# Restaging the output projection of a two-layer hybrid decoder: other buffers, an earlier fetch, a later transpose

## The chip, the cores and the metric

The kernel runs on one core of one Trainium2 chip. The core has five engines, each with an instruction queue of its own that it works through in order: TensorE (PE: matmuls and transposes into PSUM), VectorE (DVE), ScalarE (ACT), GpSimd (POOL) and SyncE (SP), which here issues every DMA. Results of TensorE land in PSUM; POOL works on SBUF alone. The metric is the device time of one execution in microseconds, as a median of several runs.

## What is computed

A sequence of 1024 tokens of width 1024 goes through two layers. Each layer normalises its input (RMSNorm), projects it into many branches, runs attention and gating on them, concatenates the gated branches to 2048 channels and multiplies by an output matrix that is added to the residual:

```python
def even_layer(h, mem, ...):
    u = rms_norm(h, norm_g)
    proj = u @ w_in
    ...
    y = jnp.concatenate([ya * jax.nn.silu(az), yb * jax.nn.silu(bz), yx * jax.nn.silu(xz)], axis=-1)
    return h + y @ w_out
```

Layer 0 (even) has eight heads of differential attention (`ya`), whose output is RMS-normalised per head, a gated short convolution (`yb`) and memory cross-attention with four heads (`yx`). Layer 1 (odd) has twelve heads of forgetting attention and the same cross-attention. The part that matters here is the last line of each layer, `h + y @ w_out`, a product of 1024 x 2048 by 2048 x 1024, and, between the layers, the RMSNorm of its result, which is the input of layer 1.

## The kernel before

All large products are made in three float32r matmuls: each operand is split into a high part (ACT, L127) and a low remainder (DVE or POOL, L128), and high x high, high x low and low x high are added up in one PSUM bank.

**Order.** The program is written as a sequence of heads and units, and a planner at build time orders each engine's queue by priority and by its own simulated times. The order of each queue is therefore fixed before the run; what stands at the head of a queue and has to wait holds up all that stands behind it. Buffers with the same tag in a pool form a ring: the next tile of a tag waits until the oldest one has been read for the last time.

**Places.** Pools lie one behind another in SBUF. `pa` holds small rings shared by everything: `raw` (4 tiles of 128x512: weights as loaded, and more), `wfh` and `wfl` (3 each), `hs` (3). `up` holds `u`, the normalised, transposed input of a layer in high and low part, four tiles of 16 KB per partition. `p1` (attention tiles) and `pw` (the token units' weights `wqh`, `wql`, 8 each) exist once per layer; between the two layers, and after the second, the pool `p2` of the output projection takes their places.

**The end of a layer's first part.** `x_pair` (two cross-attention heads at a time, called twice) runs a token unit (eight blocks of 128 tokens against `wqh`/`wql`), then two gate units, which read `u` for the last time, then the attention. The gated outputs of all heads go to DRAM (`y_dr`, 2048 x 1024, channel-major).

**The output projection** (`out_proj`, L732) works on 512 output columns at a time.
- Half 0: the weights for columns 0 to 511, 16 chunks of 128x512, are loaded through `raw` and split (`out_weights`, L691) into the places of `u`, which the layer no longer needs. The token blocks go in four pairs. For each pair and each j of 0 to 3 (512 channels) the operand `yr` (128x4x128) is loaded from `y_dr` (L713). In layer 0, for j < 2, the attention heads' norm factors `rn` are loaded as well, each row spread over all partitions (L716), and POOL multiplies them in (L717). Then `yr` is split into `yh` and `yl`, and 12 matmuls follow per block and j (L724 to L726). `yr`, `rn` and the weights all take tiles of the one ring `raw`. After the matmuls the residual `rs` is added (L745) and the result goes to DRAM. Beside this the weights of half 1 are loaded through tiles of `p2` (tags `hb` and `xn`) and split into 32 tiles `wo`.
- Half 1: the same for columns 512 to 1023, one block at a time, from the `wo` tiles. After a block's matmuls DVE adds the residual (L759), the result is stored (L760), and in layer 0 the first half of the row is loaded back (L762) and `norm_block` normalises the block for layer 1: a square sum on ACT (L134), the reciprocal root on POOL (L119, L121), the scaling on DVE (L136), eight transposes on TensorE (L141) and the split into `u`.

After layer 0's projection, layer 1 begins with the token unit of its first head, whose weights also come through `raw` and are split into `wqh`, `wql`; its first block needs the whole of the first token block of `u`, its eighth the last.

Of the kernel before, what the change touches and what calls it, by code (L numbers as in the profile page):

```python
# [7 lines left out]
F32 = mybir.dt.float32  # L8
F32R = mybir.dt.float32r
# [6 lines left out]
P = 128  # L16
# [17 lines left out]
class Trunk:  # L34
    def __init__(self, ctx, tc, io):
# [3 lines left out]
        self.up = ctx.enter_context(tc.tile_pool(name="up", bufs=1))  # L39
        self.pa = ctx.enter_context(tc.tile_pool(name="pa", bufs=1))  # L40
        self.st = ctx.enter_context(tc.tile_pool(name="st", bufs=4))
        self.ps = ctx.enter_context(tc.tile_pool(name="ps", bufs=2, space=PSUM))
# [15 lines left out]

        self.queue, self.groups, self.boot = [], 0, True
        self.attb, self.gorder = 3, (3, 2, 1, 0)  # L60
# [68 lines left out]

    def norm_block(self, src, gb, xn, dst_hi, dst_lo):  # L130

        nc = self.nc
        ms = self.st.tile([P, 8], F32, name="nb_ms")
        nc.scalar.activation(out=xn, in_=src, func=AF.Square, scale=1.0 / 32.0, accum_out=ms[:, 0:1])  # L134
        r = self.rstd(ms[:, 0:1], 1)
        nc.vector.scalar_tensor_tensor(out=xn, in0=src, scalar=r, in1=gb, op0=ALU.mult, op1=ALU.mult)  # L136
        for j in range(2):
            tp = self.bank("pt", "t")
            for i in range(4):
                c = 4 * j + i  # L140
                nc.tensor.transpose(tp[:, i * P:(i + 1) * P], xn[:, c * P:(c + 1) * P], self.ident)  # L141
# [36 lines left out]
    def token_unit(self, weights, lhs_hi, lhs_lo, nblk, post, together=False):  # L178
# [5 lines left out]
        for t0 in range(0, nblk, step):  # L184
# [40 lines left out]
    def gate_unit(self, w, c0, own=None):  # L225

        nc = self.nc
        if own is None:
            gate = {half: self.p1.tile([P, 512], F32, name="gate", tag="gate", bufs=2) for half in (1, 0)}
        else:  # L230
            gate = {half: own[:, half * 512:(half + 1) * 512] for half in (1, 0)}
# [77 lines left out]
    def mem_norm(self, layer, mem, g):  # L309
        nc = self.nc  # L310
        gb = self.p1.tile([P, T + 4], F32, name="mgb", tag="c1", bufs=1)[:, :D]
        nc.sync.dma_start(out=gb, in_=g.broadcast_to([P, D]))
# [6 lines left out]
        for b in range(2):  # L319
            x = self.p1.tile([P, T], F32, name="mx", tag="E1", bufs=self.e1b)  # L320
            nc.sync.dma_start(out=x, in_=mem[b * P:(b + 1) * P, :])
            xn = self.p1.tile([P, T], F32, name="mxn", tag="bias", bufs=1)
            with self.tc.high_priority(PRIO_EVAC):
# [210 lines left out]
    def conv_group(self, g, w):  # L534

        nc = self.nc
        ch = self.p1.tile([P, T + 4], F32, name="ch", tag="c1", bufs=1)
        nc.vector.memset(ch[:, 0:2], 0.0)
# [108 lines left out]
    def fox_head(self, h, w):  # L647
# [11 lines left out]
        if h == 0:  # L659
            self.forget_gates(fl)  # L660
        ck = self.p1.tile([P, T], F32, name="ck", tag="bias", bufs=1)
        nc.sync.dma_start(out=ck, in_=self.cum_dr[h:h + 1, :].broadcast_to([P, T]))
# [38 lines left out]

    def out_blocks(self, layer, tbs, half, tiles, res, fetch=None):

# [3 lines left out]
        for j in range(4):  # L707
            if fetch is not None:
                fetch(range(4 * j, 4 * j + 4))
            for tb, ps in zip(tbs, pss):  # L710
                ts = slice(tb * P, (tb + 1) * P)
                yr = self.pa.tile([P, 4, P], F32, name="yr2", tag="raw", bufs=4)
                nc.sync.dma_start(out=yr, in_=self.y_dr[layer][j * 512:(j + 1) * 512, ts].rearrange("(c p) t -> p c t", p=P))  # L713
# [19 lines left out]
    def out_proj(self, layer, w, res, dst, g_next):  # L733
        nc, tc = self.nc, self.tc
        with tc.tile_pool(name=f"p2_{layer}", bufs=1, reuse_waits="tile") as p2:

            self.new_u()
            u = self.u
            w0 = lambda part, c: u[part][c // 8][:, c % 8, :]
            ws = [[p2.tile([P, 512], F32R, name=f"wo{p}_{c}") for c in range(16)] for p in range(2)]  # L740
            w1 = lambda part, c: ws[part][c]
            for tbs in ((tb, tb + 1) for tb in range(0, NB, 2)):
                fetch = (lambda cs: self.out_weights(w, 0, w0, cs, self.raw_tile)) if tbs[0] == 0 else None
                for tb, (ps, rs) in zip(tbs, self.out_blocks(layer, tbs, 0, w0, res, fetch)):
                    nc.vector.tensor_tensor(out=rs, in0=ps, in1=rs, op=ALU.add)  # L745
                    nc.sync.dma_start(out=dst[tb * P:(tb + 1) * P, :512], in_=rs)
                    raws = lambda: p2.tile([P, D], F32, name="wraw", tag=("hb", "xn")[tb % 2], bufs=2)[:, :512]
                    self.out_weights(w, 1, w1, range(2 * tb, 2 * tb + 2), raws)

            if g_next is not None:  # L750
                gb = p2.tile([P, D], F32, name="gb2")
                nc.sync.dma_start(out=gb, in_=g_next.broadcast_to([P, D]))
                self.new_u()
            for tb in range(NB):
                ts = slice(tb * P, (tb + 1) * P)
                hb = p2.tile([P, D], F32, name="hb", bufs=2)
                xn = p2.tile([P, D], F32, name="xn", bufs=2)
                ((ps, rs),) = self.out_blocks(layer, [tb], 1, w1, res)
                nc.vector.tensor_tensor(out=hb[:, 512:], in0=ps, in1=rs, op=ALU.add)  # L759
                nc.sync.dma_start(out=dst[ts, 512:], in_=hb[:, 512:])  # L760
                if g_next is not None:
                    nc.sync.dma_start(out=hb[:, :512], in_=dst[ts, :512])  # L762
                    self.norm_block(hb, gb, xn, *self.u_dst(tb))


    def run(self, out):
        nc, tc, io = self.nc, self.tc, self.io
        mem = io["mem"][0]
        with tc.tile_pool(name="p1_0", bufs=1) as self.p1, tc.tile_pool(name="pw_0", bufs=1) as self.pw:
            gb = self.p1.tile([P, T], F32, name="gb", tag="bias", bufs=1)  # L770
            self.new_u()
# [14 lines left out]
            def first():  # L786
# [4 lines left out]
                for _ in (*kv, *kv1):  # L791
                    pass
                self.bias = self.p1.tile([P, T], F32, name="abias", tag="bias", bufs=1)
                nc.gpsimd.iota(self.bias, pattern=[[1, T]], base=-(NB - 1) * P, channel_multiplier=-1, allow_small_or_imprecise_dtypes=True)
                nc.gpsimd.affine_select(out=self.bias, in_=self.bias, pattern=[[-1, T]], compare_op=ALU.is_ge, fill=NEG,
                                        base=(NB - 1) * P, channel_multiplier=1)
            for h in range(8):
# [3 lines left out]
                next(conv)  # L801
            for pr in range(2):
                self.x_pair(0, pr, w, 6144, 6656)
        self.out_proj(0, io["e_w_out"][0], io["x"][0], self.h_dr, io["o_norm_g"])
        with tc.tile_pool(name="p1_1", bufs=1, reuse_waits="tile") as self.p1, tc.tile_pool(name="pw_1", bufs=1, reuse_waits="tile") as self.pw:
# [3 lines left out]
            for h in range(12):  # L809
                self.fox_head(h, w)  # L810
            for pr in range(2):
                self.x_pair(1, pr, w, 6156, 6668)
        self.out_proj(1, io["o_w_out"][0], self.h_dr, out, None)
# [31 lines left out]
```

## Time and profile before

| | us |
|---|---|
| three runs, median | 2254.02 |
| lowest, highest | 2251.73, 2256.43 |
| the profiled execution | 2251.72 |
| its span, first to last instruction | 2249.9 |

The profile shows one execution. Its page gives for each engine the busy time, a picture of the span in 40 slices, the DMA queues, the chain of work that ended last, and the costliest groups of instructions. Behind the page stand views of the trace: the waits (who waited for whom, in total, how often, longest), tables of chosen stretches (busy time and instructions of each engine, the clock granted to TensorE as a share of full speed, DMA share and rate), groups by line within a stretch, and timelines. In a timeline a row gives start, length, engine, line, operation and tiles, and in brackets how long the engine stood idle before it and what ended that. Matmuls overlap, so the time per matmul is read from the distance of two starts.

### The profile page before, as it was taken

The page shows a single profiled execution, that of the slowest core. Times are in us where ns is not written, and L with a number is a line of the kernel's source. Part 1 is how long each engine was busy: PE and PEld are TensorE (multiplying, and loading weights), DVE is VectorE, ACT ScalarE, POOL GpSimd, SP SyncE. Part 2 cuts the span into 40 slices and gives each one's busy share as a digit, 9 for nine tenths or more (in the row PEclk, how much of TensorE's full clock was granted, in tenths as well). Part 3 has the DMA queues.
Part 4 walks back from the last instruction along what each step waited for, and adds up shares of the span by engine and source line. Part 5 has one row for each costly group of instructions (what it writes and reads, how often), then busy time and mean ns, then how long its engine had stood idle before and what let it go on. Part 6 is the DMA issues. An engine that isn't in the chain of part 4 may idle for free. (4 is left out here: it accounts for less than half of the span.)

```text
span 2249.9 us, 35841 instructions
## 1 busy us (share of the span) xinstructions
PE 2182.4 (97%) x12528; PEld 1974.7 (88%) x12528; DVE 1233.4 (55%) x2860; ACT 1057.8 (47%) x2503; POOL 1018.3 (45%) x1356
## 2 busy tenths in 40 slices
PE   7999999999999999888889999999999999999999
PEld 6889989889899899766679999999999999997887
DVE  5646756666665666542334555555555555555532
ACT  5655555465464554432234444444444444544421
POOL 4565655555555552332235555445555554522100
PEclk9999999999999999999999999999999999999999
DMA  5450210210201111585552221121222211214753
GB/s 162 126 159 19 61 56 17 70 47 23 71 27 44 51 59 36 168 243 161 137 144 54 57 53 36 40 55 48 55 57 57 57 40 38 61 55 137 222 155 98
DMA packets 266076, 183.06 MB, mean 81 GB/s; under 512 B 24572, under 2 KB 242844, under 8 KB 265896
## 3 DMA queue, kind: packets, MB, share of 16 engines
q1 hardware_dynamic: 265896, 180.77, 28.3%
q8 instruction: 99, 1.62, 0.3%
q14 instruction: 81, 0.66, 0.1%
HBM read 153.32 MB, written 27.38 MB: 80 GB/s over the span
## 5 line engine op out<-in xcount | busy, mean ns | idle before, releaser
L189 PE MATMUL pd<-wqh,u 128*128 128x384 f32 (+2 forms) x1536 | 513.7, 335 | 0.6 <-ACT wqh L127 0.5
L190 PE MATMUL pd<-wql,u 128*128 128x384 f32 (+2 forms) x1536 | 512.1, 334 | 0.0
L191 PE MATMUL pd<-wqh,u 128*128 128x384 f32 (+2 forms) x1536 | 511.4, 333 | 0.0
L189 PEld LDWEIGHTS pd<-wqh,u 128*128 128x128 f32 x1536 | 290.2, 189 | 4.9 <-ACT u L127 0.8
L190 PEld LDWEIGHTS pd<-wql,u 128*128 128x128 f32 x1536 | 290.2, 189 | 4.9 <-POOL wql L128 0.2
L191 PEld LDWEIGHTS pd<-wqh,u 128*128 128x128 f32 x1536 | 290.0, 189 | 4.3
L220 PE MATMUL pd<-u,wfh 128*128 128x512 f32 x704 | 277.9, 395 | 0.0
L219 PE MATMUL pd<-u,wfl 128*128 128x512 f32 x704 | 277.5, 394 | 0.0
L218 PE MATMUL pd<-u,wfh 128*128 128x512 f32 x704 | 277.2, 395 | 0.0
L128 POOL TENSOR_TENSOR wql<-raw,wqh 128x384 fp32r<-128x384 f32 (+2 forms) x220 | 217.0, 997 | 89.0 <-ACT wqh L127 83.7
L258 DVE TENSOR_TENSOR qr<-qr,rs_r 128x256 f32<-128x256 f32 x200 | 137.3, 687 | 106.7 <-POOL rs_r L121 105.2
L127 ACT ACTIVATE yh<-yr 128x512 fp32r<-128x512 f32 x128 | 79.9, 629 | 235.4 <-POOL yr L717 124.2
L121 POOL TENSOR_TENSOR rs_r<-rs_v,neghalf 128x2 f32<-128x2 f32 (+2 forms) x220 | 177.7, 809 | 14.1
L127 ACT ACTIVATE pth<-pt 128x512 fp32r<-128x512 f32 (+1 forms) x232 | 121.9, 555 | 130.1 <-PE pt L411 128.0
L673 POOL TENSOR_TENSOR fbias<-ck,cqn 128x896 f32<-128x896 f32 (+3 forms) x96 | 110.3, 1149 | 156.4 <-DVE mx L394 123.6
L128 DVE TENSOR_TENSOR yl<-yr,yh 128x512 fp32r<-128x512 f32 x128 | 89.7, 706 | 164.0 <-ACT yh L127 158.3
L127 ACT ACTIVATE wqh<-raw 128x384 fp32r<-128x384 f32 (+2 forms) x256 | 118.4, 481 | 125.4 <-DMA raw<-in_e_w_in_dram 62.6
L128 POOL TENSOR_TENSOR wfl<-rawf,wfh 128x512 fp32r<-128x512 f32 x88 | 119.4, 1358 | 106.1 <-ACT wfh L127 105.8
L128 DVE TENSOR_TENSOR ptl<-pt,pth 128x512 fp32r<-128x512 f32 (+1 forms) x232 | 143.7, 639 | 42.9 <-ACT pth L127 40.8
L128 POOL TENSOR_TENSOR vl<-qr,vh 128x128 fp32r<-128x128 f32 x160 | 80.6, 510 | 175.0 <-ACT vh L127 168.0
L220 PEld LDWEIGHTS pd<-u,wfh 128*128 128x128 f32 x704 | 132.4, 188 | 27.3 <-issue 0.6
L219 PEld LDWEIGHTS pd<-u,wfl 128*128 128x128 f32 x704 | 132.4, 188 | 26.4 <-issue 1.4
(239 smaller groups left out, 4992.4 us busy)
## 6 DMA issues: line engine op xcount, KB each, us to landing
yr<-y_dr SPq DMA_DIRECT2D x128, 256.0 KB
raw<-in_o_w_in_dram SPq DMA_DIRECT2D x288, 64.0 KB
rawf<-in_e_w_in_dram SPq DMA_DIRECT2D x56, 256.0 KB
y_dr<-y SPq DMA_DIRECT2D x112, 128.0 KB
raw<-in_e_w_in_dram SPq DMA_DIRECT2D x192, 64.0 KB
wraw<-in_e_w_out_dram SPq DMA_DIRECT2D x32, 256.0 KB
rn<-on_dr SPq DMA_DIRECT2D x32, 256.0 KB
rawf<-in_o_w_in_dram SPq DMA_DIRECT2D x32, 256.0 KB
```

The lines of the kernel that those rows point to most:

```text
L121: nc.gpsimd.tensor_tensor(out=r[:, :n], in0=v[:, :n], in1=self.neghalf[:, :n], op=ALU.pow)
L127: nc.scalar.activation(out=hi, in_=src, func=AF.Copy)
L128: lo_eng.tensor_tensor(out=lo, in0=src, in1=f32(hi), op=ALU.subtract)
L189: nc.tensor.matmul(ps[:, :n], lhsT=ah(k), rhs=h, start=(k == 0), stop=False)
L190: nc.tensor.matmul(ps[:, :n], lhsT=ah(k), rhs=l, start=False, stop=False)
L191: nc.tensor.matmul(ps[:, :n], lhsT=al(k), rhs=h, start=False, stop=(k == KC - 1))
L218: nc.tensor.matmul(ps, lhsT=h, rhs=uh[:, k, :], start=(k == 0), stop=False)
L219: nc.tensor.matmul(ps, lhsT=l, rhs=uh[:, k, :], start=False, stop=False)
L220: nc.tensor.matmul(ps, lhsT=h, rhs=ul[:, k, :], start=False, stop=(k == KC - 1))
L258: nc.vector.tensor_tensor(out=v, in0=v, in1=r.unsqueeze(2).broadcast_to([P, ng, gs]), op=ALU.mult)
L673: nc.gpsimd.tensor_tensor(out=b[:, :kext], in0=ck[:, :kext], in1=self.cqn[:, qb, h:h + 1].broadcast_to([P, kext]), op=ALU.subtract)
```

## The change

- Tiles with tags `c1`, `bias`, `gate`, `kd` and `kz` move from `p1` to a pool `pk` that lives through both layers (all uses; one is shown).
- `out_early`, called between the two calls of `x_pair` in both layers, loads and splits the first five weight chunks of half 0 into the places of `kd`, `kz`, `c1` and `bias`, which have no other use at that time. Only eleven chunks then go into `u`.
- `yr` and `rn` leave `raw` and get rings of their own in `p2`, of 5 and 4 tiles. A tile `gap` that nothing uses shifts them to the end of `p2`.
- The weights of half 1 go through `raw`; `hb` becomes two named tiles, `gb2` is allocated ahead of them, and `xn` uses `bias` and `c1` in turn.
- `norm_block` is cut in two, `norm_rows` and `turn_rows`. In half 1 a block's `turn_rows` (transposes and split) comes after the matmuls of the next block, that of the last block after the third block of the next layer's first token unit. The load of the row's first half comes ahead of the block's matmuls.

```diff
+    def norm_rows(self, src, gb, xn):
...
+    def turn_rows(self, xn, dst_hi, dst_lo):
...
+    def norm_block(self, src, gb, xn, dst_hi, dst_lo):
+        self.norm_rows(src, gb, xn)
+        self.turn_rows(xn, dst_hi, dst_lo)
...
     def token_unit(...)
                 with self.tc.high_priority(PRIO_EVAC):
                     post(tb, ps)
+            if self.turn_last is not None and t0 == 2:
+                self.turn_last()
+                self.turn_last = None
             self.tick()
...
     def att_half(self, name):
-        return self.p1.tile([P, 512], F32R, name=name, tag=name, bufs=self.attb)
+        pool = self.pk if name in ("kd", "kz") else self.p1
+        return pool.tile([P, 512], F32R, name=name, tag=name, bufs=self.attb)
...
+    def out_early(self, w):
+
+        early = [[], []]
+        for i in range(3):
+            for part, n in enumerate(("kd", "kz")):
+                early[part].append(self.att_half(n))
+        for t in ("c1", "bias"):
+            two = self.pk.tile([P, T + 4] if t == "c1" else [P, T], F32R, name="we", tag=t, bufs=1)
+            for part in range(2):
+                early[part].append(two[:, part * 512:(part + 1) * 512])
+        self.early = early
+        self.out_weights(w, 0, lambda part, c: early[part][c], range(len(early[0])), self.raw_tile)
...
     def out_blocks(...)
-                yr = self.pa.tile([P, 4, P], F32, name="yr2", tag="raw", bufs=4)
+                yr = pool.tile([P, 4, P], F32, name="yr2", tag="yr", bufs=5)
...
-                    rn = self.pa.tile([P, 4, P], F32, name="rn", tag="raw", bufs=4)
+                    rn = pool.tile([P, 4, P], F32, name="rn", tag="rn", bufs=4)
...
     def out_proj(...)
-            u = self.u
-            w0 = lambda part, c: u[part][c // 8][:, c % 8, :]
+            u, early = self.u, self.early
+            ne = len(early[0])
+            w0 = lambda part, c: early[part][c] if c < ne else u[part][(c - ne) // 8][:, (c - ne) % 8, :]
             ws = [[p2.tile([P, 512], F32R, name=f"wo{p}_{c}") for c in range(16)] for p in range(2)]
             w1 = lambda part, c: ws[part][c]
+
+            gb = p2.tile([P, D], F32, name="gb2")
+            hbs = [p2.tile([P, D], F32, name=f"hb{i}") for i in range(2)]
+            p2.tile([P, 784], F32, name="gap")
...
-                    raws = lambda: p2.tile([P, D], F32, name="wraw", tag=("hb", "xn")[tb % 2], bufs=2)[:, :512]
-                    self.out_weights(w, 1, w1, range(2 * tb, 2 * tb + 2), raws)
+                    self.out_weights(w, 1, w1, range(2 * tb, 2 * tb + 2), self.raw_tile)
...
+            turn = None
             for tb in range(NB):
                 ts = slice(tb * P, (tb + 1) * P)
-                hb = p2.tile([P, D], F32, name="hb", bufs=2)
-                xn = p2.tile([P, D], F32, name="xn", bufs=2)
-                ((ps, rs),) = self.out_blocks(layer, [tb], 1, w1, res)
+                hb = hbs[tb % 2]
+                if g_next is not None:
+                    nc.sync.dma_start(out=hb[:, :512], in_=dst[ts, :512])
+                ((ps, rs),) = self.out_blocks(layer, [tb], 1, w1, res, p2)
+                if turn is not None:
+                    turn()
                 nc.vector.tensor_tensor(out=hb[:, 512:], in0=ps, in1=rs, op=ALU.add)
                 nc.sync.dma_start(out=dst[ts, 512:], in_=hb[:, 512:])
                 if g_next is not None:
-                    nc.sync.dma_start(out=hb[:, :512], in_=dst[ts, :512])
-                    self.norm_block(hb, gb, xn, *self.u_dst(tb))
+                    t = ("bias", "c1")[tb % 2]
+                    xn = self.pk.tile([P, T + 4] if t == "c1" else [P, T], F32, name="xn2", tag=t, bufs=1)[:, :D]
+                    self.norm_rows(hb, gb, xn)
+                    turn = lambda xn=xn, tb=tb: self.turn_rows(xn, *self.u_dst(tb))
+            self.turn_last = turn
...
             for pr in range(2):
+                if pr == 1:
+                    self.out_early(io["e_w_out"][0])
                 self.x_pair(0, pr, w, 6144, 6656)
```

More of the change, by code (lines that the diff above doesn't have):

```diff
@@ L228, in gate_unit @@
         if own is None:
-            gate = {half: self.p1.tile([P, 512], F32, name="gate", tag="gate", bufs=2) for half in (1, 0)}
+            gate = {half: self.pk.tile([P, 512], F32, name="gate", tag="gate", bufs=2) for half in (1, 0)}
         else:
@@ L536, in conv_group @@
         nc = self.nc
[L537 removed]
+        ch = self.pk.tile([P, T + 4], F32, name="ch", tag="c1", bufs=1)
         nc.vector.memset(ch[:, 0:2], 0.0)
@@ L700, in raw_tile, with out_blocks @@
         return self.pa.tile([P, 512], F32, name="wraw", tag="raw", bufs=4)
-    def out_blocks(self, layer, tbs, half, tiles, res, fetch=None):
+    def out_early(self, w):
[9 more added lines that the diff above has]
+        self.out_weights(w, 0, lambda part, c: early[part][c], range(len(early[0])), self.raw_tile)
+    def out_blocks(self, layer, tbs, half, tiles, res, pool, fetch=None):
         nc = self.nc
```

22 lines of the change are left out of this document (12 added, 10 removed).

## The prediction

> **What bounds the kernel now.** I read the page's busy shares first, then TensorE's waits in each layer's late part, then a table of stretches.
>
> ```profile
> span 2249.9 us, 35841 instructions
> PE 2182.4 (97%) x12528; PEld 1974.7 (88%) x12528; DVE 1233.4 (55%) x2860; ACT 1057.8 (47%) x2503; POOL 1018.3 (45%) x1356
> ...
> PE pd L724 <- ACT yh L127: 22.6, 9, 4.1
> PE pt L141 <- DVE xn L136: 14.4, 6, 4.1
> PE pd L726 <- DVE yl L128: 2.6, 3, 1.3
> ...
> PE pd L724 <- ACT yh L127: 2.3, 2, 1.2
> ```
>
> TensorE (PE) is the bound, idle for 67.5 us of the span. The first three waits are all that it has between 900 and 1260 us (layer 0's output projection), the last line all between 1990 and 2250 us (layer 1's). So 39.6 us of the idle time lies in one stage, whose stretches are the first three rows here (the other rows serve as yardsticks; columns: busy us and instructions of PE, weight load, DVE, ACT, POOL, granted clock, DMA share, GB/s):
>
> ```profile
> 917.00:959.00 42.00, 39.35 (x194) 32.98 (x195) 25.86 (x61) 21.29 (x52) 14.80 (x11) 0.88 0.64 184
> 959.00:1037.70 78.70, 70.44 (x288) 54.74 (x287) 29.56 (x41) 24.43 (x41) 24.74 (x19) 0.96 0.76 221
> 1037.70:1172.00 134.30, 109.40 (x442) 85.42 (x441) 42.14 (x60) 35.63 (x65) 30.05 (x35) 0.91 0.52 143
> ...
> 2156.00:2246.00 90.00, 90.00 (x387) 72.24 (x385) 25.55 (x38) 18.97 (x30) 0.00 (x0) 1.00 0.41 124
> ...
> 2060.00:2080.00 20.00, 17.57 (x96) 14.09 (x94) 13.80 (x26) 11.19 (x24) 5.50 (x5) 1.00 0.67 206
> ...
> 2120.00:2140.00 20.00, 20.00 (x90) 16.57 (x89) 10.59 (x14) 8.94 (x15) 5.18 (x4) 1.00 0.80 252
> ```
>
> They are the first pair of token blocks (mixed with the end of the attention), the other three pairs of half 0, and half 1. Layer 1's half 1, with the same 384 matmuls, takes 90 us without a gap at clock 1.00; layer 0's takes 134.3 at 0.91. A gap costs twice: its own length, and the slow matmuls behind it. The chain behind one gap, from the timelines of POOL, ACT, DVE and PE:
>
> ```profile
> 1091.95 0.68 DVE L759 TENSOR_TENSOR hb<-pd,rs 128x512 f32<-128x512 f32 x1
> ...
> 1092.66 1.06 ACT L134 ACTIVATE xn<-hb 128x1024 f32<-128x1024 f32 x1 [1.06 <-DVE hb L759]
> ...
> 1097.16 1.26 POOL L717 TENSOR_TENSOR yr<-yr,rn 128x512 f32<-128x512 f32 x1 [7.71 <-DMA rn<-on_dr]
> 1098.51 0.22 POOL L119 TENSOR_SCALAR rs_v<-nb_ms 128x1 f32<-128x1 f32 x1
> 1098.81 0.57 POOL L121 TENSOR_TENSOR rs_r<-rs_v,neghalf 128x1 f32<-128x1 f32 x1
> ...
> 1099.41 1.28 DVE L136 SCALAR_TENSOR_TENSOR xn<-hb,rs_r,gb 128x1024 f32<-128x1024 f32 x1 [6.18 <-POOL rs_r L121]
> ...
> 1100.85 1.94 PE L141 MATMUL pt<-ident,xn 128*128 128x128 f32 x8 [4.11 <-DVE xn L136]
> ...
> 1103.01 0.63 PE L724 MATMUL pd<-wo,yh 128*128 128x512 f32 x1
> ...
> SPq L713 <- DMA rn<-on_dr: 48.4, 17, 4.2
> ```
>
> The square sum is ready by 1093.9, but POOL, in order, stands on L717, which waits for a norm factor (rn) still in flight; the norm and the eight transposes start about 5 us late, and the matmuls behind run 0.63 us each. The root is in the last row (SP's own waits, 900 to 1180): the next operand load (L713) cannot be issued until an older rn has gone through, since both share four raw buffers. So this is a shortage of buffers, not of bandwidth: half 1 moves 143 GB/s.
>
> **The change part by part.** What can be won, against TensorE's own rate:
>
> ```profile
> 1010.13 0.39 PE L724 MATMUL pd<-u,yh 128*128 128x512 f32 x1
> ...
> 1015.80 0.39 PE L725 MATMUL pd<-u,yh 128*128 128x512 f32 x1
> ...
> 2190.02 0.40 PE L724 MATMUL pd<-wo,yh 128*128 128x512 f32 x1
> ...
> 2195.86 0.39 PE L725 MATMUL pd<-wo,yh 128*128 128x512 f32 x1
> ...
> 880.00 0.28 PE L190 MATMUL pd<-wql,u 128*128 128x256 f32 x1
> 880.12 0.28 PE L191 MATMUL pd<-wqh,u 128*128 128x256 f32 x1
> ...
> 917.30 0.80 PE L724 MATMUL pd<-u,yh 128*128 128x512 f32 x1 [4.12 <-ACT yh L127]
> ...
> 1083.79 1.07 PE L141 MATMUL pt<-ident,xn 128*128 128x128 f32 x8 [0.26 <-DVE xn L136]
> 1084.62 0.48 PE L726 MATMUL pd<-wo,yl 128*128 128x512 f32 x1
> ```
>
> The first two pairs of rows stand 25 matmuls apart each: one per 0.227 us in half 0 and 0.234 in half 1; a 256-wide one takes 0.12, eight transposes 0.83. Then:
> - first pair, 913.2 (917.30 less the 4.12 us wait) to 959: 45.8 us. Of its 194 instructions some 104 are wide (96 of the pair, a few of the next), 90 narrow: 23.6 + 10.8 = 34.4. Loss 11.4.
> - the rest of half 0: 78.7 us for 288, all wide but six: 64.0 + 0.7. Loss 14.0.
> - half 1: 134.3 us for 442, of which 56 are transposes: 386 x 0.234 + 7 x 0.83 = 96.1. Loss 38.2.
> - layer 1: the 2.3 us of waits.
>
> In all 66 us is the most that can go.
>
> Own rings for yr (5) and rn (4). Half 1 needs per block four yr, two rn, rs, hb and the store (the DMA view's issues from 1037 to 1180 us):
>
> ```profile
> yr<-y_dr SPq DMA_DIRECT2D x29, 256.0 KB
> rn<-on_dr SPq DMA_DIRECT2D x14, 256.0 KB
> h_dr<-hb SPq DMA_DIRECT2D x8, 256.0 KB
> rs<-in_x_dram SPq DMA_DIRECT2D x7, 256.0 KB
> hb<-h_dr SPq DMA_DIRECT2D x7, 256.0 KB
> ```
>
> That is nine times 256 KB (2.36 MB) per block of 48 x 0.234 + 0.9 = 12.1 us: 195 GB/s, where layer 1 ran at 252 without a gap. Five yr are a block and a quarter ahead, 5 x 2.8 = 14 us, against the 7.71 us wait above. Then neither POOL nor DVE stands, and the chain from the block's end to xn is 0.68 + 1.06 + 0.22 + 0.57 + 1.28, about 4.5 us with what lies between, inside the next block's 11.2. I count 33 of the 38.2, leaving about 0.65 us a block. Bounds: 0 (the waits only move) and 38.2. The hb load, counted above, moves ahead of its block's yr loads and is not needed before the block's end.
>
> The rest of half 0 is harder. The same row's share, 0.76 of 78.7, is 59.8 us of fully busy DMA engines; in 64.7 us that would be a share of 0.92. The highest share above with a gap-free PE is 0.80, at which the stretch takes 74.8 us and wins 4. Deeper rings smooth it, and the first pair has room. I take 6, between 0 and 14.0.
>
> Early chunks and early places. Five of 16 weight chunks of half 0 are fetched and split during the last x pair: per layer five DMAs past SP's y stores, 5 x 0.6 us of ACT (the row at 906.23: 1.16 for two), 2 x 0.7 of DVE and 3 x 1.3 of POOL (by L759 and L717, 128x512 as well). Cover:
>
> ```profile
> 880.00:900.00 20.00, 20.00 (x127) 17.90 (x126) 6.37 (x14) 6.02 (x13) 4.09 (x7) 1.00 0.04 14
> ...
> 906.23 1.16 ACT L127 ACTIVATE u<-wraw 128x512 fp32r<-128x512 f32 x2 [2.76 <-PE pd L219]
> ...
> 908.81 0.37 SPq L713 DMA_DIRECT2D yr<-y_dr  x1
> ...
> 888.34 0.28 PE L191 MATMUL pd<-wqh,u 128*128 128x256 f32 x1
> ```
>
> There PE is full and everything else at a third or less, so I cost the fetch at nothing; without cover it is at most POOL's 3.9 us. Now the first split waits for the gate units to leave u (906.23), and the first yr is issued at 908.81. By tile sizes in order of allocation the new rings lie where the token unit's weights wqh and wql lay, last read at 888.34, so loads can go 20 us sooner. The 4.12 us wait should go, with its slow stretch: I take 7 of 11.4, between 0 and 11.4. Layer 1: 2 of 2.3.
>
> The moves of gate, kd, kz, c1 and bias into a pool of their own change places only; nothing. Half-1 weights now pass through the raw ring instead of four p2 buffers: the same number, off yr's path; nothing.
>
> Transposes one block later: L141 at 1100.85 already stands behind 47 of the next block's 48 matmuls (the row at 1084.62, an L726, is the 48th of its block, behind the transposes). The move passes one matmul: nothing by itself, its wait goes with the rings. The last block's turn moves behind three blocks of layer 1's first unit; the waits above show none there.
>
> What is late next: the rings lie over wqh and wql of layer 1 too.
>
> ```profile
> L128 POOL TENSOR_TENSOR wql<-raw,wqh 128x384 fp32r<-128x384 f32 (+2 forms) x220 | 217.0, 997 | 89.0 <-ACT wqh L127 83.7
> ```
>
> The last yr is split three steps (3 x 12 x 0.234 = 8.4 us) before half 1 ends; eight wql take 8 x 1.0 = 8.0 us on POOL, and the first half of them has older slots. Nothing, at worst 8.4 us.
>
> The sum: 7 + 6 + 33 + 2 = 48 us. The profiled execution took 2251.7 (span 2249.9 and 1.8 around it): 2203.7. The three runs' median is 2.3 above it, so 2254.0 - 48 = **2206**.
>
> The 0.92 above is the row that speaks loudest against the change. The Trainium skill (Perfetto Trace Analysis, DMA Optimizations) has a rule with it: small DMAs, under 2 KB, carry significant overhead, and yr and rn come in 512-byte rows. By that rule the transfers' rate is the limit, the rings win nothing in half 0, and the sum is the first rival's, 2219.
>
> The gaps that I leave cost only themselves: the stretch 2060 to 2080 holds layer 1's two waits, the longest 1.2 us, at clock 1.00. The Trainium skill (TensorE: Matmul & The Clock Gate, Part 1) has the clock fall only after an idle window of about 3.4 us, which agrees; were it otherwise, leftover gaps would cost about twice, some 5 us more.
>
> **The rivals.**
> - Half 0 stays bound by transfers: only half 1 and layer 1 gain, 33 + 2. 2219 (2214 to 2224). For it: the share of 0.92. Against: 252 GB/s beside a full PE. 0.18.
> - The wait moves: POOL still takes L717 as loads land, in an order fixed before the run, so L119 stands behind one that isn't there. Half of half 1 (17) and 6 elsewhere: 2231 (2224 to 2249). For it: POOL's order is unchanged. Against: the ring's lead. 0.11.
> - It doesn't do what it says: SP, one queue, issues in an order that gives the rings no lead. 2254, within 0.2% (4.5 us, what a measurement of this kernel can tell from no change). 0.04.
> - Slower: a yr load issued for a slot not yet free stands at SP's head, and rs, hb, stores and the next layer's weights stand behind it, in both layers. Layer 0 loses its 63 us as now; layer 1's 16 block passes, all but gap-free today, each lose a 2 us landing: 2254 + 32 = 2286. It decides once the mean loss over both layers' 32 block passes is above 66 / 32 = 2.1 us. For it: SP already waits 48.4 us at L713. Against: slots come free steps ahead. 0.05.
>
> The forecast (2188 to 2214) has 0.62.
>
> **How the numbers follow.** Low end: all 66 us gone, 2254.0 - 66 = 2188. High end: past the first rival and into the second, 2232; left out are the rest of the second, the third and the fourth, under 0.2. Faster 0.62 + 0.18 + 0.11 = 0.91, same 0.04, slower 0.05.
>
> **What would show it.** Right: layer 0's half 1 near 101 us at clock 0.98 or more; POOL's wait for rn gone ahead of L119; PE's L141 wait for xn gone; first L724 with no 4 us wait; DMA share in half 0 above 0.85. Wrong: PE still waiting for yh with SP at L713; a wait for wqh at layer 1's start; waits in layer 1's half 1.

## The result, and the profile after the change

The changed kernel takes 2290.07 us (median of four runs, 2288.14 to 2293.37), the kernel before 2255.22 beside it: ratio 1.0156, 95% interval 1.0134 to 1.0178. The forecast of 2206 us, its range up to 2232 and its sign were wrong. Layer 0's half 1 hardly gained, and both layers' projections begin late. Medians are of the fast executions alone; one of rings_early_rep below, 2643.77 us at a granted clock of 0.75, is left out.

From the page of the changed kernel: span, busy time of the engines, and in 40 slices TensorE's busy tenths and the granted clock.

```profile
span 2291.6 us, 35847 instructions
...
PE 2198.5 (96%) x12528; PEld 1983.2 (87%) x12528; DVE 1241.3 (54%) x2860; ACT 1060.1 (46%) x2503; POOL 1023.6 (45%) x1356
...
PE   7999999999999999797889999999999999998999
...
PEclk9999999999999999799999999999999999999999
```

TensorE's idle time grew from 67.5 to 93.1 us and its busy time from 2182.4 to 2198.5, and the seventeenth slice (917 to 974 us, the start of layer 0's projection) has a clock of 0.7. Moments of both traces, in us from the start of each span, show where the spans part. Each is the start of the matmul named, an end being the start of the last one. The two profiled executions are 41.7 us apart, the medians 34.9: the table shows places, and its sizes are those of one execution each.

| moment | before | after | apart |
|---|---|---|---|
| last gate matmul, layer 0 | 911.3 | 914.9 | +3.6 |
| first projection matmul, layer 0 | 917.3 | 950.8 | +33.5 |
| end of half 0 | 1037.7 | 1051.1 | +13.4 |
| end of half 1 | 1171.8 | 1182.5 | +10.7 |
| first gate matmul, layer 1 | 1208.8 | 1232.3 | +23.5 |
| last gate matmul, layer 1 | 2052.4 | 2079.4 | +27.0 |
| first projection matmul, layer 1 | 2053.5 | 2108.1 | +54.6 |
| end of half 0, layer 1 | 2156.2 | 2197.5 | +41.3 |
| end of half 1, layer 1 | 2245.8 | 2287.4 | +41.6 |

Three places lose: the start of each layer's projection (+9.8 and +14.3 from the last gate matmul to the end of half 0) and the start of layer 1 (+12.8). Half 1 of layer 0, where 33 us were to be won, won 4.2 between its first and its last matmul, and 2.7 with the wait ahead of its first one. The heads ahead of the two projections take 3.6 and 3.5 us longer as well; why is not settled.

**The starts.** SP's own rows of the changed kernel, first around layer 0's projection, then around layer 1's (start, duration, what is issued, how many):

```profile
928.67 12.76 SPq L442 DMA_DIRECT2D y_dr<-y  x6
941.52 0.39 SPq L739 DMA_DIRECT2D yr<-y_dr  x1
...
2091.72 12.37 SPq L442 DMA_DIRECT2D y_dr<-y  x6
2104.18 2.68 SPq L739 DMA_DIRECT2D yr<-y_dr  x5
```

In both layers the first operand load stands behind the last six y stores of the attention, which come as attention ends. In the kernel before, the first yr left at 908.81, in the middle of the attention, whose gaps the projection's matmuls then filled. SP's order is fixed when the kernel is built, so a free slot of the ring is of no use here.

**The start of layer 1.** ACT's rows of the changed kernel:

```profile
1184.06 1.06 ACT L135 ACTIVATE xn<-hb 128x1024 f32<-128x1024 f32 x1
...
1185.10 1.79 ACT L128 ACTIVATE wqh<-raw 128x396 fp32r<-128x396 f32 x4
```

The first weight split of layer 1 follows the last norm, after half 1's last matmul (1182.5); the first token-unit matmul comes at 1190.0.

**Half 1.** The table of stretches of the changed kernel (columns as in the prediction), half 0 and half 1:

```profile
950.80:1051.10 100.30, 93.08 (x383) 72.41 (x384) 38.29 (x44) 26.10 (x43) 29.04 (x22) 0.97 0.74 209
1052.80:1182.50 129.70, 107.03 (x434) 82.88 (x435) 43.59 (x60) 32.94 (x57) 24.16 (x29) 0.92 0.49 130
```

The two largest waits of all engines in its half 1 (total, times, longest):

```profile
POOL yr L743 <- DMA yr<-y_dr: 85.7, 7, 17.3
DVE xn L137 <- POOL rs_r L122: 43.0, 7, 9.2
```

POOL no longer waits for rn but for yr, about 12 us a block, and the norm's small operation still stands behind it in POOL's order. Two queues of the changed kernel over one block say why; SP's rows first, then POOL's:

```profile
1102.74 0.36 SPq L742 DMA_DIRECT2D rn<-on_dr  x1
1103.51 0.36 SPq L739 DMA_DIRECT2D yr<-y_dr  x1
1103.99 0.43 SPq L742 DMA_DIRECT2D rn<-on_dr  x1
...
1107.94 1.84 SPq L739 DMA_DIRECT2D yr<-y_dr  x2
1118.78 0.36 SPq L742 DMA_DIRECT2D rn<-on_dr  x1
...
1101.43 2.54 POOL L743 TENSOR_TENSOR yr<-yr,rn 128x512 f32<-128x512 f32 x2 [12.44 <-DMA yr<-y_dr]
1117.46 2.51 POOL L743 TENSOR_TENSOR yr<-yr,rn 128x512 f32<-128x512 f32 x2 [12.53 <-DMA yr<-y_dr]
```

SP issues nine transfers within 7 us, then stands for 9 us until POOL's multiplication frees an rn slot; POOL waits for the yr at the end of that burst. The loop takes 16.0 us where the prediction counts 12.1 for TensorE. It is as long as the burst takes to land, and that is where the rn loads come in (the run after_rep).

### The profile page after: what moved, and what is told of

The parts are those of the page before. It is cut to its first block, busy times and chain, and to the rows that moved or that the text cites. A ratio compares the mean times of both kernels' runs of the same rounds, so it can differ in the third digit from the quotient of the medians.

```text
span 2291.6 us, 35847 instructions
## 1 busy us (share of the span) xinstructions
PE 2198.5 (96%) x12528; PEld 1983.2 (87%) x12528; DVE 1241.3 (54%) x2860; ACT 1060.1 (46%) x2503; POOL 1023.6 (45%) x1356
## 4 chain that ended last, share of the span: by engine, by line
PE 45%; DMA 4%; POOL 2%; DVE 1%; issue 1%; ACT 1%; SPq 0%; POOLq 0%; DVEq 0%; ACTq 0%
PE pd L198 6%; PE pd L200 6%; PE pd L199 6%; PE pss L390 4%; PE pd L750 3%; PE pd L752 3%; PE pd L751 3%; DMA yr<-y_dr 3%; PE pd L230 2%; PE pd L231 2%; PE pd L232 2%; PE pt L424 2%; PE po L438 1%; PE po L437 1%; PE po L436 1%; PE pt L279 1%
## 5 line engine op out<-in xcount | busy, mean ns | idle before, releaser
L129 DVE TENSOR_TENSOR yl<-yr,yh 128x512 fp32r<-128x512 f32 x128 | 95.9, 756 | 173.9 <-ACT yh L128 173.6
```

What stands on the lines that cost most here:

```text
L129: lo_eng.tensor_tensor(out=lo, in0=src, in1=f32(hi), op=ALU.subtract)
```

## The experiments

Two causes were in question: the place of the rings, through the order that it gives SP and layer 1's weights, and the rn transfers, 256 KB read out of four 512-byte pieces by all 128 partitions. The traces give, in us: from layer 0's last gate matmul to the end of half 0; half 1, from its first to its last matmul; from there to layer 1's first matmul (the column "join"); from layer 1's last gate matmul to the end of its half 0. Between half 0 and half 1 lie 0.2 to 0.3 us, but 1.7 in the changed kernel, 0.9 in before_rings, and 5.1 and 5.0 in rings_back and rings_back_long.

| kernel | median us | ratio to before, 95% | half 0 | half 1 | join | half 0, layer 1 |
|---|---|---|---|---|---|---|
| before | 2255.2 | | 126.4 | 133.9 | 0.2 | 103.8 |
| changed | 2290.1 | 1.0134 to 1.0178 | 136.2 | 129.7 | 7.5 | 118.1 |
| rings_back | 2284.3 | 1.0120 to 1.0161 | 140.4 | 127.5 | 0.7 | 110.5 |
| rings_back_long | 2293.4 | 1.0161 to 1.0195 | 142.3 | 121.8 | 7.5 | 112.5 |
| before_rings | 2288.4 | 1.0138 to 1.0183 | 136.6 | 121.2 | 7.5 | 123.5 |
| after_rep | 2245.1 | 0.9947 to 0.9977 | 122.1 | 97.0 | 7.4 | 119.8 |
| before_rep | 2208.2 | 0.9786 to 0.9815 | 114.6 | 101.4 | 0.2 | 104.3 |
| rings_early | 2236.7 | 0.9910 to 0.9943 | 126.1 | 110.7 | 0.7 | 102.4 |
| rings_early_rep | 2209.9 | 0.9796 to 0.9829 | 113.9 | 96.6 | 0.7 | 105.8 |
| turn_later | 2249.3 | 0.9977 to 0.9996 | 124.7 | 130.3 | 0.7 | 103.4 |
| early_w | 2258.6 | 1.0015 to 1.0034 | 126.6 | 126.5 | 0.7 | 101.7 |
| early_w_rep | 2204.2 | 0.9769 to 0.9798 | 108.5 | 96.4 | 0.7 | 102.3 |
| before_rep_turn | 2204.6 | 0.9773 to 0.9802 | 114.7 | 96.3 | 0.7 | 104.3 |
| rn_2k | 2214.4 | 0.9807 to 0.9840 | 115.2 | 104.6 | 0.3 | 104.6 |

### before_rings: the rings alone

```diff
-                yr = self.pa.tile([P, 4, P], F32, name="yr2", tag="raw", bufs=4)
+                yr = pool.tile([P, 4, P], F32, name="yr2", tag="yr", bufs=5)
...
-                    rn = self.pa.tile([P, 4, P], F32, name="rn", tag="raw", bufs=4)
+                    rn = pool.tile([P, 4, P], F32, name="rn", tag="rn", bufs=4)
```

> The kernel before with one edit: yr2 and rn get rings of five and four slots in p2. No early weight chunks, no later transposes, no buffers moved to pk. Late-start theory: all yr2 loads stand behind the last y store, in both layers, and p2 now reaches over layer 1's weight tiles; the first projection matmul of layer 0 comes at 940 to 952 us for 917.3, and the time is 2270 to 2295 us, 15 to 40 above before. Rival (the rings are sound and another edit makes the loss): 2225 to 2256 us, half 1 of layer 0 well below 133.9 us.

Measured: 2288.4 us, first projection matmul at 951.0. The rings alone bring the whole loss. Half 1 does win 12.7 us by them (133.9 to 121.2), less than the starts and the way into layer 1 cost.

### rings_back and rings_back_long: the rings out of p2 again

```diff
-                yr = pool.tile([P, 4, P], F32, name="yr2", tag="yr", bufs=5)
+                yr = self.pa.tile([P, 4, P], F32, name="yr2", tag="raw", bufs=4)
...
-                    rn = pool.tile([P, 4, P], F32, name="rn", tag="rn", bufs=4)
+                    rn = self.pa.tile([P, 4, P], F32, name="rn", tag="raw", bufs=4)
...
-            p2.tile([P, 784], F32, name="gap")
```

> The changed kernel with yr2 and rn taken from the shared four-slot raw ring again, as before the change, and with the gap tile dropped, so that p2 ends below the weight tiles of layer 1. All other edits stay. Late-start theory: tiles of p2 are planned only when the pools on whose bytes p2 lies are closed, so in the changed kernel every yr2 and rn load stands in SP's order behind the last y store of attention. In raw they stand among those stores: the first projection matmul of layer 0 moves from 950.8 us to 917 to 925, that of layer 1 from 2108.1 to about 2056, and with p2 short layer 1's weight splits start before half 1 has ended. Worth about 10 (start of layer 0) + 13 (start of layer 1's heads) + 14 (end): 2246 to 2262 us. Rival (the early weight chunks, or the transposes one block later, cause the loss): the time stays at 2283 to 2295. Rival (own buffers do help half 1 and are now lost): half 1 of layer 0 grows from 129.7 us to 134 or more.

> As the run with the rings back in raw, but the gap tile is made longer (5392 elements for 784), so that p2 ends where it ends in the changed kernel, over the weight tiles of layer 1, though nothing uses these bytes. Theory that the overlap alone delays layer 1's weight splits until the last user of p2: layer 1's first token-unit matmul comes 8 to 15 us later against the end of half 1 than in the run with the short pool, and the time is 8 to 15 us above it. Rival (only real users of the same bytes hold the splits back; the late start came from the transposes one block later): no difference beyond 3 us between the two.

rings_back_long differs from rings_back in one thing: it keeps the unused gap tile and makes it 5392 elements long. SP's rows of rings_back:

```profile
909.03 0.38 SPq L442 DMA_DIRECT2D y_dr<-y  x1
914.15 0.37 SPq L739 DMA_DIRECT2D yr<-y_dr  x1
915.87 0.37 SPq L742 DMA_DIRECT2D rn<-on_dr  x1
```

The loads stand among the y stores again; first matmuls at 918.1 and 2076.2, 0.3 us behind their gates in each layer. The order followed the rings' pool, as expected, but the time did not: 2284.3 us. Half 0 took 140.4 us, since yr2, rn and both halves' weights now shared four raw slots; early_w below tests this.

The pair prices the overlap with layer 1's weight tiles. First weight split of layer 1 in rings_back, then in rings_back_long with the norm ahead of it (ACT's rows):

```profile
1181.73 0.53 ACT L128 ACTIVATE wqh<-raw 128x396 fp32r<-128x396 f32 x1 [5.13 <-DMA raw<-in_o_w_in_dram]
```

```profile
1188.37 1.06 ACT L135 ACTIVATE xn<-hb 128x1024 f32<-128x1024 f32 x1
...
1189.41 1.79 ACT L128 ACTIVATE wqh<-raw 128x396 fp32r<-128x396 f32 x4
```

With the pool ending below these tiles, the first split runs ahead of half 1's last matmul (1190.8); with an unused tile stretching the pool over them, it comes behind p2's last norm, as in the changed kernel. The difference is 2293.4 - 2284.3 = 9.2 us with the medians unrounded, and no instruction of the projection reads or writes the bytes that make it. In the profiled executions the way from half 1's last matmul to layer 1's first gate matmul takes 38.3 us in rings_back and 49.8 in rings_back_long, as in the changed kernel (before: 37.0); rings_back gives 4 us of that back ahead of it, as its half 1 ends later. The wait for layer 1's first matmul alone grew by 6.8 us, a little less than the 8 to 15 expected.

### after_rep and before_rep: quick rn loads

```diff
+        self.on_rep = self.dr.tile([8, P, T], F32, name="on_rep")
...
+        nc.sync.dma_start(out=self.on_rep[h], in_=self.on_dr[h:h + 1].broadcast_to([P, T]))
...
-                    nc.sync.dma_start(out=rn, in_=self.on_dr[4 * j:4 * j + 4, ts].unsqueeze(0).broadcast_to([P, 4, P]))
+                    nc.sync.dma_start(out=rn, in_=self.on_rep[4 * j:4 * j + 4, :, ts].rearrange("c p t -> p c t"))
```

> The changed kernel, rings and all, with one edit: after each attention head its row of norm factors is copied to 128 rows of a scratch buffer in HBM, and an rn load reads for each partition its own row instead of the same four 512-byte pieces for all 128 partitions. Bytes, pieces and order of the rn loads are as in the changed kernel; eight copies of 512 KB are added during the heads. Theory that rn loads are slow because all partitions read the same pieces: an rn load falls from 4 to 5 us of queue time to about 1, half 1 of layer 0 from 129.7 us to 97 to 112 and half 0 by 0 to 15, less 0 to 8 for the copies: 2245 to 2272 us. Rival (an rn load is slow as any load of 512-byte pieces, or half 1 is held by the fixed order of SP, not by the transfer): half 1 stays at 124 to 132 us, the time at 2283 to 2300.

> The kernel before with one edit, the row of norm factors copied to 128 rows of a scratch buffer after each head, and rn read from these. Buffers, order and everything else as before. Theory that layer 0's projection waits for slow rn transfers and not for slots: half 1 of layer 0 falls from 133.9 us to 97 to 112 although yr2, rn and nothing else share the four raw slots, half 0 from 119.8 us to 100 to 114; 2208 to 2235 us. Rival (slots: four slots for yr2 and rn hold half 1 whatever an rn load costs, as the prediction argued): half 1 stays at 120 us or more and the time at 2236 to 2254.

Measured: 2245.1 and 2208.2 us, about 45 us less in each. The DMA view of the two kernels over the same part of a block, beginning with rn, yr, rn: the changed kernel from 1103.5 to 1110.0, then after_rep from 1089.5 to 1092.5.

```profile
DMA packets 1428, 0.73 MB, mean 112 GB/s; under 512 B 34, under 2 KB 1423, under 8 KB 1427
...
q1 hardware_dynamic: 1427, 0.72, 52.7%
```

```profile
DMA packets 1508, 0.80 MB, mean 268 GB/s; under 512 B 42, under 2 KB 1474, under 8 KB 1508
...
q1 hardware_dynamic: 1508, 0.80, 91.3%
```

About as many bytes in pieces of the same size took 6.5 us with rn from one place and 3.0 with rn from rows of their own: 3.5 us a block, and by an estimate from this one block 8 x 3.5 = 28 of the 32.7 us by which half 1 became shorter. The last line of each view has the DMA engines' busy share: 53% in the slow window and 91% in the quick one. The slow loads left the engines idle for half of the time, so a low share and a low rate were no sign of room to spare. POOL's rows of after_rep show the loop of 16.0 us closed in 10.9, within the 12.1 of TensorE:

```profile
1076.29 2.55 POOL L745 TENSOR_TENSOR yr<-yr,rn 128x512 f32<-128x512 f32 x2 [8.13 <-DMA yr<-y_dr]
...
1087.22 2.56 POOL L745 TENSOR_TENSOR yr<-yr,rn 128x512 f32<-128x512 f32 x2 [7.42 <-DMA yr<-y_dr]
```

The stretches of after_rep, half 0 and half 1, the latter at clock 1.00:

```profile
947.30:1036.80 89.50, 89.39 (x384) 73.49 (x385) 41.78 (x47) 27.63 (x45) 33.06 (x23) 0.97 0.85 246
1037.00:1134.00 97.00, 95.69 (x436) 77.07 (x435) 41.60 (x57) 32.19 (x56) 23.79 (x28) 1.00 0.55 163
```

The kernel before tells more. Its stretches with quick rn and nothing else changed:

```profile
916.50:1027.60 111.10, 104.81 (x479) 84.75 (x480) 60.74 (x103) 46.03 (x92) 41.64 (x31) 0.97 0.77 233
1027.80:1129.20 101.40, 97.74 (x441) 78.69 (x440) 42.02 (x58) 34.89 (x62) 28.58 (x33) 0.98 0.62 181
```

Half 1 runs in 101.4 us although yr2 and rn share four raw slots. With quick loads four slots were enough (before_rep_turn below, with the same four, comes to 96.3).

### rings_early and rings_early_rep: rings in a pool that is always open

```diff
+        kk = name in ("kd", "kz")
+        return pool.tile([P, 512], F32R, name=name, tag="kk" if kk else name, bufs=6 if kk else self.attb)
...
-                yr = pool.tile([P, 4, P], F32, name="yr2", tag="yr", bufs=5)
+                yr = self.pk.tile([P, 4, P], F32, name="yr2", tag="kk", bufs=6)
...
-                    rn = pool.tile([P, 4, P], F32, name="rn", tag="rn", bufs=4)
+                    rn = self.pk.tile([P, 4, P], F32, name="rn", tag="gate", bufs=2)
...
-                if pr == 1:
-                    self.out_early(io["e_w_out"][0])
```

(The same call of layer 1 and the gap tile are gone too.)

> The changed kernel with the rings in places whose pool is open since the start: yr2 takes six slots in pk where kd and kz lay, rn two where the gate lay; so there are no early weight chunks, and no gap, and p2 ends below layer 1's weight tiles. Transposes one block later, xn in the places of bias and c1 and half 1's weights through raw as in the changed kernel. rn as before, slow. Late-start theory: first projection matmul of layer 0 at 915 to 928 us for 950.8, of layer 1 within 5 us of its last gate matmul for 28.7 us, the weights of layer 1 in time; half 1 of layer 0 still 124 to 132 us, as rn sets it. 2236 to 2262 us. Rival (rings of their own lose in half 0 wherever they lie, through contention on the DMA queue): 2270 us or more.

> As the run before, and rn from the replicated rows. If the late start and the slow rn are the two causes and independent, their gains add: half 1 of layer 0 at 97 to 104 us, half 0 at 90 to 105 us from a start at 915 to 928 us: 2195 to 2222 us, below every other kernel here. Rival (the early start only moves the wait, since attention and the first weight splits end when they did): 2225 to 2245 us.

Measured: 2236.7 and 2211.7 us. Starts and join are sound (first matmul at 916.8; layer 1's 0.3 us behind its gate). Half 1 with slow rn was not as expected: 110.7 us, not 124 to 132. Slots or their order do count while rn is slow: six and two in an order that starts early do more than the changed kernel's five and four (129.7); which of the two it is, order or count, the runs do not settle. With quick rn half 1 takes 96.6 against 101.4 in before_rep, but this kernel has the later transposes too, and before_rep_turn below comes to 96.3 by these alone, so the rings bring nothing that shows. Half 0 took 113.9 us where 90 to 105 were expected, and the whole, expected below every other kernel, is no faster than before_rep (2209.9 for 2208.2).

### turn_later, early_w, early_w_rep, before_rep_turn: the small edits

turn_later, on the kernel before:

```diff
                 ((ps, rs),) = self.out_blocks(layer, [tb], 1, w1, res)
+                if tb and g_next is not None:
+                    turn()
...
-                    self.norm_block(hb, gb, xn, *self.u_dst(tb))
+                    self.norm_rows(hb, gb, xn)
+                    turn = lambda xn=xn, tb=tb: self.turn_rows(xn, *self.u_dst(tb))
+            if g_next is not None:
+                turn()
```

> The kernel before with one edit: in half 1 of layer 0 a block's transposes are issued after the next block's projection matmuls; the last block's stay in place. Theory (rn sets the pace of half 1): the wait for xn that goes from ahead of the transposes comes back ahead of the next block's matmuls, half 1 at 126 to 134 us, 2246 to 2256 us. Rival (the wait for xn is a cost of its own): half 1 at 122 us or less, 2238 to 2245 us.

early_w, on rings_back:

```diff
-                    self.out_weights(w, 1, w1, range(2 * tb, 2 * tb + 2), self.raw_tile)
+                    two = p2.tile([P, D], F32, name="wraw2", tag="hb", bufs=2)
+                    raws = iter((two[:, :512], two[:, 512:]))
+                    self.out_weights(w, 1, w1, range(2 * tb, 2 * tb + 2), lambda: next(raws))
```

> The run with the rings back in raw (2284 us), with one edit: half 1's weight chunks are loaded into the two hb tiles of p2, as before the change, and no longer through raw. What is left of the change is then the eight early weight chunks and the transposes one block later. Theory (in the run with the rings back, half 0 took 140.1 us because yr2, rn and both halves' weights shared four raw slots): half 0 falls to 114 to 124 us, layer 1's half 0 by about 7 us, 2244 to 2258 us. Rival (the early chunks themselves make half 0 slow, since their loads and splits run amid attention): half 0 at 132 us or more and 2268 to 2286 us.

(The text speaks of eight early chunks; the diff fetches five.)

The other two are early_w and turn_later with the diff of quick rn on top.

> As the run before, and rn from the replicated rows. Against the kernel before with replicated rows (2208.2 us) it adds the early chunks and the later transposes. Theory (the prediction's: early chunks cost nothing and bring what the first pair loses to its weights): half 0 at 104 to 110 us for 111.1, half 1 at 97 to 99 us for 101.4, 2196 to 2206 us. Rival (early chunks bring nothing, as the tensor engine has attention's work in that time anyway): half 0 at 110 to 116 us, 2204 to 2214 us.

> The kernel before with the replicated rows and the transposes one block later, nothing else. With rn cheap the wait for xn ahead of the transposes is the next one in line: half 1 of layer 0 at 96.5 to 99 us for 101.4, 2202 to 2207 us for 2208.2. Rival (the wait comes back elsewhere, as when only the transposes were moved): 2207 to 2212 us.

Transposes later bring 2.9 us by the interval's middle (0.9987), and half 1 is 96.3 us for 101.4 once rn is quick. Half 1's weights through raw cost 2284.3 - 2258.6 = 25.7 us when yr2 and rn are in raw too, in half 0 of both layers and in the wait between half 0 and half 1. With them out of the way the rest of the change, above all five early chunks and the later transposes, is 5.3 us slower than before with slow rn, with half 0 at 126.6 us where 114 to 124 were expected; its last gate matmul comes 7.9 us later (919.2), and why is not settled. With quick rn the kernels with and without the chunks are 0.5 us apart: half 0 is 6 us shorter in the profiled execution, but the median shows no gain that can be told from none.

### rn_2k: what makes the loads slow

```diff
+        self.on_blk = self.dr.tile([NB, 8, P], F32, name="on_blk")
...
+        nc.sync.dma_start(out=self.on_blk[:, h, :], in_=self.on_dr[h].rearrange("(n p) -> n p", p=P))
...
-                    nc.sync.dma_start(out=rn, in_=self.on_dr[4 * j:4 * j + 4, ts].unsqueeze(0).broadcast_to([P, 4, P]))
+                    nc.sync.dma_start(out=rn, in_=self.on_blk[tb, 4 * j:4 * j + 4, :].unsqueeze(0).broadcast_to([P, 4, P]))
```

> The kernel before with one edit: after each head its row of norm factors is also copied into a buffer in HBM whose order is block, head, token, so that the four rows of an rn load are 2 KB in one piece. All 128 partitions still read the same 2 KB, but in 128 pieces and not in 512. It asks what makes an rn load slow. Theory A (many pieces from one place, each with its own cost): with a fourth of the pieces half 1 of layer 0 falls from 133.9 us to 99 to 108, as with the replicated rows (101.4), 2206 to 2222 us. Theory B (256 KB out of one place of HBM take their time, however cut): half 1 stays at 124 us or more, 2240 to 2256 us.

Measured: 2214.4 us, half 1 in 104.6:

```profile
1029.30:1133.90 104.60, 98.16 (x440) 78.17 (x439) 40.73 (x58) 34.66 (x62) 28.55 (x33) 0.98 0.60 176
```

A fourth of the pieces from the same place recovers nearly all of it. The cost hangs mostly on the number of pieces read from one place, not on the bytes alone. (The four rows of a load also lie in one stretch here, where they stood 4 KB apart; that part is not separated.) The Trainium skill (Perfetto Trace Analysis, DMA Optimizations) says that DMAs under 2 KB carry significant overhead. This run agrees, if a piece is taken as such a DMA, for pieces out of one place; for places of their own no run here shows it, and the 512-byte pieces of after_rep moved at 268 GB/s.

## Why the prediction was wrong, point by point

The issue of the rn for which POOL waits in the prediction's chain, in SP's rows of the kernel before:

```profile
1090.86 0.36 SPq L716 DMA_DIRECT2D rn<-on_dr  x1
```

A short gap in the same half 1, and matmuls behind it, in PE's rows of the kernel before:

```profile
1133.61 1.07 PE L141 MATMUL pt<-ident,xn 128*128 128x128 f32 x8 [1.97 <-DVE xn L136]
...
1135.06 0.63 PE L725 MATMUL pd<-wo,yh 128*128 128x512 f32 x1
1135.49 0.63 PE L726 MATMUL pd<-wo,yl 128*128 128x512 f32 x1
```

- **"This is a shortage of buffers, not of bandwidth."** This step failed for half 1. It was read from a mean of 143 GB/s, and the 195 GB/s that the rings would need was set against 252 in layer 1, whose blocks have no rn. But the wait quoted, 7.71 us for a 256 KB load, was for the most part a transfer in flight: SP had issued that rn at 1090.86 (the row above), and POOL took it at 1097.16. A quick rn takes 32.5 us from half 1 in the kernel before and 32.7 in the changed one, nearly the 33 forecast, and the first needs no ring. So the prediction had the size of the loss in half 1 right and its cause wrong. The rings without a quick rn gave 12.7 (before_rings) to 23 (rings_early, with the later transposes), in the changed kernel 4.2 with its other edits.
- **"So loads can go 20 us sooner."** This step failed for the starts. Whether the bytes were free did not count, since the operands were not issued: SP's order put them behind the last y store. Half 0 lost 9.8 us in layer 0, where 13 were to be won, and 14.3 in layer 1, where 2 were. That the order follows the pool, not the bytes, is shown: rings in raw or pk have it right, the same rings in p2 alone have it wrong. That the builder places a pool's tiles only after the users of older pools on its bytes is my reading of these orders.
- **"What is late next: nothing, at worst 8.4 us."** The right place, but too small and by a wrong route: I counted real users of the bytes. The overlap costs 9.2 us with no user in the projection at all, and in the changed kernel layer 1's first gate matmul comes 12.8 us further behind.
- **Edits at nothing.** The later transposes are worth 3 us, though forecast at nothing by themselves: the L726 at 1084.62 was read as the 48th matmul of its block, and counted from the start of half 1 it is the 39th, so the move passes ten matmuls (2.3 us at 0.234), not one. The early chunks bring nothing that can be measured with quick rn; with slow rn early_w is 9 us above turn_later, and whether the chunks make that is not settled. Half 1's weights through raw, put at nothing as off yr's path, cost 25.7 us where yr2 and rn are in raw as well; what they cost beside rings of their own no run shows.
- **"The gaps that I leave cost only themselves."** This was read from waits of up to 1.2 us at clock 1.00. The idle window of about 3.4 us that the Trainium skill (TensorE: Matmul & The Clock Gate, Part 1) gives was taken to agree. The second group of rows above does not: behind an idle time of 1.97 us the matmuls start 0.43 us apart for 0.23 ahead of it, and the granted clock from 1134.9 to 1138.0 is 0.50. The measurement decides: here a gap well under 3.4 us cost more than itself.
- **The rivals.** The fourth, at 0.05, had the sign, and its 2286 for 2290 is luck, as its mechanism is only half there: SP does stand behind a slot, in layer 0 alone; in layer 1 half 1 is 89.7 us long and full. The second was there as well, 43 us of DVE behind POOL's order. None had a late first load. The first, transfers in half 0, was near the truth for the wrong load: quick rn takes 11.8 us off half 0 of the kernel before.
- **The signs.** Half 1 at 101 us with a clock of 0.98 is what before_rep shows. The changed kernel showed two of the signs named for wrong: waits for yh, and layer 1's weights late. Of those named for right it showed one, as POOL no longer waits for rn; it waits for yr in its place, and the norm behind it is late as before.

Placement and rn each count without the other. after_rep and early_w_rep, both with quick rn, differ by the place of yr2 and rn and by the half-1 buffers only: 2245.1 - 2204.2 = 41 us. The same two with slow rn, the changed kernel and early_w, are 31.5 apart.

before_rep_turn and early_w_rep, at 2204.6 and 2204.2 us, beat both kernels; the first is the kernel before with two small edits, quick rn and later transposes.

## What to carry to other kernels

Before giving a stalled load more slots, see how long one load is in flight and at what rate its bytes move: a slow transfer in a shared queue looks like a shortage of slots. After moving a buffer to another pool, read the order of the issuing queue in the new build, not only the addresses: a free byte is no permission to issue. Where every partition reads the same row, try it in HBM in longer pieces or in several copies; here both took away most of the cost.

## What the runs showed of the hardware

Reads by all 128 partitions of the same four 512-byte pieces ran at 112 GB/s with their neighbours in the queue, the same sizes from rows of their own at 268 GB/s, 2.4 times as fast, and the yr loads behind them in the queue landed late (POOL waited 85.7 us for yr in half 1 of the changed kernel). The DMA engines' busy share was 0.53 in the slow window and 0.91 in the quick one. Writing 128 copies of each row took eight copies of 512 KB during the heads. No cost of these shows: the last matmul of layer 0's last token unit came 1.7 us later in before_rep (890.0 for 888.3) and 0.2 us earlier in after_rep (891.7 for 892.0).
